# A two-part transformer in one launch: all steps placed anew, with one reader per PSUM bank and powers in gaps of VectorE; 14 identity transposes in place of 32

## The chip, the core and the metric

The kernel runs on one core of one Trainium2 chip. The metric is the device time of one launch in microseconds (us). The kernel before takes 2158.5 us in the median of three runs (2158.13 to 2163.83).

## What is computed

Two blocks follow each other on the same 512 tokens of width 1024, all in float32. Cut to what matters:

```python
# first block, layer 0: differential attention beside a memory attention
h = rms_norm(x, a_norm); q, k, v, qm, gate = split(h @ a_w_in)
q, k = rope(rms_norm(q)), rope(rms_norm(k))            # per head of 64
o = (softmax(q0 k0') - lam * softmax(q1 k1')) @ v      # causal, 6 heads of 128
x = x + (concat(rms_norm(o), mem_attention(qm, mem)) * silu(gate)) @ a_w_out
# first block, layer 1: stick-breaking attention, 12 heads of 64
k, v = split(rms_norm(x, kv_norm) @ w_kv_shared); q, qm, gate = split(rms_norm(x, b_norm) @ b_w_in)
x = x + (concat(stick_breaking(q, k, v), mem_attention(qm, mem)) * silu(gate)) @ b_w_out
# second block, two layers of the same form
proj = rmsnorm(x) @ w_in                               # 1024 to 12 parts
y_a = gmlp_spatial(u, v) * silu(z_a)
y_b = mla_attention(c_q, c_kv, k_rope) * silu(z_b)     # 8 heads, latent queries and keys
y_c = rg_lru(x_c) * silu(z_c)                          # convolution, two gates, a scan over time
m = sigmoid(g_a)*(y_a @ w_proj_a) + sigmoid(g_b)*(y_b @ w_proj_b) + sigmoid(g_c)*(y_c @ w_proj_c)
x = x + rmsnorm(m @ w_out)
```

## The kernel before

**Products.** Every float32 matrix is split into a rounded part and the rest (`split`: `hi` is a copy that rounds, `lo` is the source less `hi`), and each product is three matmuls, hi by hi, hi by lo and lo by hi (`mm3`). Weights come by DMA in chunks of 512 KB or less into the arena `fa` (float32), are split there into the arena `ra` (the rounded type), and are then used; the split is a copy on ScalarE or VectorE and a subtraction on VectorE (`wchunk`, `dense_fm`, `dense_tm`, `dense_tk`). The arena `sm` holds small columns. The eight PSUM banks are `ps0` to `ps7`.

**Steps.** A block is a set of named steps, run in the order of a list: in the first layer `q0` to `q2` are the three groups of queries and keys, `v0` and `v1` the values (with the memory's queries in `v1`), `h0` to `h5` the heads, `k0` and `k1` the memory's keys and values of both layers, `a0` the memory attention, `n0` the norm over the heads, `g0` to `g7` the gates, `f0` to `f7` the gated products. In the second layer `p0` to `p5` are pairs of heads. In the second block `Q0` makes the rotated parts of all eight heads' queries, `T0` to `T7` are the heads, `Z`, `G`, `z` gates, `R` the recurrence, and `A`, `B`, `D` the three projections.

**Order.** Nothing is issued while the steps run: `Sched.record` only notes each operation, with what it reads and writes. `Sched.place` then goes through a model of five engines with costs written out by hand (`cost`) and gives each engine, whenever it is free in the model, the first operation that is ready, so that the order on all engines, the tiles' places in memory, and for operations marked with `any` also the engine (a copy on ScalarE or VectorE, a product of two tiles on VectorE or GpSimd) come out of it. Tables steer it: the step lists `plan_a`, `plan_b`, `plan_l`, `plan_l1`; how far ahead of the oldest unfinished operation a step may begin (`reach_*`, `window*`); how much earlier its weights may be asked for (`lead_*`); and `spare` (PSUM banks kept free), `hold`, `early`, `depth`, `patience`. `Sched.issue` emits the result, so nearly every instruction of a profile bears the one line 571 (line 600 in the changed kernel), and rows are told apart by tiles and shapes. What waits on what is set by the real dependencies: two engines that read one PSUM bank read it one after the other.

**Details that the change touches.** Where heads are normalised (`head_norm_T`), the reciprocal root is a power on GpSimd (`rpow`), and the result goes through TensorE transposes against the identity (`identr`, `ident`, tiles `rc` and `ident`). `pairs_T` stores transposed pairs of heads, the even head of each pair in one half of the partitions. At the very start 32 transposes of the identity onto itself keep TensorE busy while the first loads are under way.

Of the kernel before, what the change touches and what calls it, by code (L numbers as in the profile page):

```python
# [19 lines left out]
P = 128  # L20
# [9 lines left out]
class VTile:  # L30

    __slots__ = ("kind", "units", "cols", "at", "uses", "first", "last", "busy")

    def __init__(self, kind, units, cols):
        self.kind, self.units, self.cols = kind, units, cols
        self.at, self.uses, self.first, self.last, self.busy = None, 0, None, None, 0.0


class VAP:
# [119 lines left out]
class Sched:  # L161

    plan_l = "q0 k0 Q0 V0 N0 N1 T0 T1 Z1 T2 Z0 T3 N3 V1 N2 T4 T5 Z5 Z2 C0 Z4 Z3 T6 Z6 T7 Z7 B1 W0 X0 R1 R0 " \
        "B7 G1 G4 X1 B0 G2 G3 B2 W1 R2 G0 R3 B6 B4 B3 M0 S0 G5 G9 G6 B5 G7 M1 G8 P1 P6 D0 D7 P5 P2 P0 " \
        "z2 z0 D3 D4 P7 D5 P4 P3 z1 z3 z7 u1 u2 z4 z5 D6 z6 u0 u3 D2 u5 u6 u7 u4 A3 A6 A4 A2 A0 D1 A7 " \
        "A5 A1"
    reach_l = {'A': 1200, 'B': 300, 'D': 300, 'M': 350, 'P': 150, 'Q': 600, 'R': 1200, 'T': 200, 'V': 600, 'Z':
        800, 'u': 400, 'z': 500}  # L170
    plan_l1 = "k0 q0 V0 Q0 N1 N0 N2 T0 T2 T1 Z1 V1 Z0 N3 T6 Z2 T4 T5 Z5 T3 Z3 T7 C0 Z7 Z4 X0 Z6 W0 R1 B1 R0 " \
        "G2 M0 W1 B0 G3 B2 G1 X1 R2 B3 G4 G0 S0 B6 R3 B4 B7 G5 B5 M1 G6 P4 G7 G9 G8 D6 P3 P0 P2 D5 P7 " \
        "z2 D4 P6 z6 P1 P5 u6 z3 z4 D0 z0 u2 z5 u0 u3 u5 z7 D7 z1 u1 D1 u7 D2 u4 A5 A1 A2 D3 A6 A3 A0 " \
        "A7 A4"
    reach_l1 = {'A': 500, 'D': 150, 'M': 600, 'N': 250, 'P': 300, 'Q': 350, 'R': 150, 'S': 100, 'T': 50, 'X': 400,
        'q': 250, 'z': 1200}
    patience = 2500
    window_a = 169
    window = 169
    window_b = 200  # L180
    window_l = 298
    pool_n = 256
    reach_n = 94
    reach_x = 49
    spare = 1
    hold = 24
    early = 100
    late_x = (0, 40, 520)
    last = 1
    plan_a = "c0 q0 q2 v0 h0 h1 k0 q1 v1 g2 h2 h3 g1 h5 g6 h4 g7 n0 a0 g4 f6 f1 g0 f0 f2 f7 f4 g5 f5 g3 k1 " \  # L190
        "f3"
    plan_b = "v0 q0 p0 q1 p1 q2 m0 q3 a0 q4 q5 p2 g7 p4 g2 g1 g4 p5 g0 g6 p3 g3 g5"
    reach_a = {'a': 100, 'c': 50, 'f': 2000, 'g': 250, 'h': 50, 'm': 2250, 'n': 400, 'q': 600, 'v': 400}
    reach_b = {'a': 100, 'g': 400, 'm': 250, 'p': 400, 'q': 300}
    depth = 64
    lead_a = {'a': 20, 'f': 120, 'h': 800, 'k': 20, 'q': 120, 'v': 200}
    lead_b = {'a': 200, 'g': 120, 'm': 200, 'p': 300, 'q': 40, 'v': 500}
    lead_l = {'A': 80, 'C': 800, 'G': 200, 'P': 120, 'S': 500, 'T': 80, 'W': 200, 'X': 200, 'Z': 120, 'u': 40, 'z': 800}
    lead_l1 = {'A': 200, 'B': 80, 'D': 800, 'G': 800, 'R': 80, 'T': 80, 'X': 200, 'Z': 300, 'k': 20, 'u': 80, 'z': 80}

    def __init__(self, nc, mems):
        self.nc, self.mems = nc, mems
# [181 lines left out]
    def place(self):  # L384
# [55 lines left out]
        def pick(e, t):  # L440
            h, held, late, found = ready[e], [], None, None
            while h and len(held) < self.depth:
                x = heapq.heappop(h)
                op = ops[x[1]]
                if op.start is not None:
                    continue
                if op.idx > front + op.reach:
                    held.append(x)
                    if op.idx > front + 1500:
                        break  # L450
                    continue
# [12 lines left out]
                found = op  # L464
                break
# [25 lines left out]
        while done < len(ops):  # L491
# [11 lines left out]
            if what == "ready":  # L503
                enlist(x)
            elif what == "done":
                fin[x] = 1
                if x == front:
                    while front < len(ops) and fin[front]:
                        front += 1
                    moved = True  # L510
            elif what == "give":
                mems[x.kind].give(x)
                freed.add(x.kind)
            if events and events[0][0] <= t:
                continue
            for kd in (parked if moved else freed):
# [8 lines left out]
            for e in engs:  # L525
# [14 lines left out]
                op.start, op.eng = t, e  # L540
# [6 lines left out]
                ends[op.idx] = end  # L547
                push(end, "done", op.idx)
                done += 1
                for s in op.succ:  # L550
                    so = ops[s]
                    so.left -= 1
                    if so.left == 0:
                        so.ready = max(ends[d] + self.lat(ops[d].eng, so.alts[0][0]) for d in so.deps)
                        push(so.ready, "ready", so)
                for v in op.vts:
                    v.uses -= 1
                    v.busy = max(v.busy, end)
                    if v.uses == 0:
                        push(v.busy + 150, "give", v)  # L560
        self.span = t
        return order

# [55 lines left out]
class Kern:  # L619
# [80 lines left out]
    def consts(self):  # L700
# [178 lines left out]
    def pairs_T(self, dst, src):  # L879
# [54 lines left out]
    def mem_attention(self, qT, kT, vm):  # L934
# [4 lines left out]
        for p in range(2):  # L939
            o = self.p()  # L940
            for hh in range(2):
                lo = 64 * hh
                pT = self.r(2, 512)
                for u in range(2):
                    sc = self.p(2, 256)
                    for i in range(2):
                        for x in range(2):
                            self.mm(sc[:, i, :], qT[:, 2 * p + hh, tok(2 * u + i)], kT[x][:, 2 * p + hh, :], x == 0, x == 1)
                    m, sm = self.s(2), self.s(2)
                    nc.vector.tensor_reduce(m, sc, axis=AX.X, op=ALU.max)  # L950
                    nc.vector.tensor_scalar(m, m, -0.125, None, op0=ALU.mult)
# [444 lines left out]
    def latent(self, l, A, w, hT, lhs):  # L1396
# [427 lines left out]
```

## Time and profile before

| | value |
|---|---|
| median of three runs | 2158.5 us |
| profiled execution, its own time | 2162.5 us |
| profiled execution, its span | 2160.7 us |
| TensorE (PE) busy | 2121.9 us of the span |
| VectorE (DVE) busy | 1427.7 us |
| ScalarE (ACT) busy | 939.1 us |
| GpSimd (POOL) busy | 87.8 us |
| TensorE's granted clock, mean | 0.996 of full |

A page of the profile describes one profiled execution. A row of a group gives the line, the engine, the operation, the tiles written and read, how often, the busy time and the mean length of one, and then the idle time ahead of these instructions with what ended it. "PE ps <- DVE ra" among the waits means that TensorE stood until VectorE had written a tile of `ra`. In a table by stretch the clock column is the share of TensorE's full clock that was granted.

### The profile page before, as it was taken

Reading aid. Unit: us, or ns where it says so; the run is one execution under the profiler, and the core shown is the slowest. Engines: PE = TensorE matmul, PEld = TensorE weight load, DVE = VectorE, ACT = ScalarE, POOL = GpSimd, SP = SyncE. Lnnn points to the kernel's source line nnn. Section 1 sums busy time; section 2 is a strip of 40 time slices with the busy share of each in tenths; the row PEclk is TensorE's granted clock in tenths of the full one; section 3 lists DMA queues with packets and bytes.
Section 4 is the critical chain, followed back from the end, with each engine's and each line's share of the span. In section 5 each row is a group of like instructions: output and inputs, shape, how many; then the busy total and the mean of one; then the engine's idle time right before and its main releaser. Section 6 shows DMA issues by size and latency. Waiting matters only on the chain.

```text
span 2160.7 us, 27498 instructions
## 1 busy us (share of the span) xinstructions
PE 2121.9 (98%) x10191; PEld 1764.0 (82%) x10191; DVE 1427.7 (66%) x2761; ACT 939.1 (43%) x1706; POOL 87.8 (4%) x94
## 2 busy tenths in 40 slices
PE   9999999999999999999999999999999999999998
PEld 7877788788898888888888888888878888888887
DVE  7678966778777777874635434687886676553343
ACT  5546633555445546563412122445655454122321
POOL 1220000000010000000100000100000000000000
PEclk9999999999999999999999999999999999999999
DMA  5431353552553033633424542521435254244442
GB/s 165 117 95 52 123 182 85 129 133 73 168 146 83 12 100 104 169 93 103 124 70 126 153 138 92 173 75 38 128 87 143 76 143 124 73 141 122 134 137 78
DMA packets 325245, 243.51 MB, mean 113 GB/s; under 512 B 22565, under 2 KB 278389, under 8 KB 324726
## 3 DMA queue, kind: packets, MB, share of 16 engines
q1 hardware_dynamic: 325110, 241.75, 39.1%
q8 instruction: 80, 1.31, 0.2%
q14 instruction: 55, 0.45, 0.1%
HBM read 205.26 MB, written 16.78 MB: 103 GB/s over the span
## 4 chain that ended last, share of the span: by engine, by line
PE 63%; DVE 3%; ACT 1%; DMA 1%; issue 0%; POOL 0%; SPq 0%; DVEq 0%; POOLq 0%; ACTq 0%
PE ps L571 63%; DVE fa L571 2%; DVE ra L571 1%; ACT ra L571 0%; ACT fa L571 0%; DMA fa<-in_w_in 0%; DMA ra<-ra 0%; POOL sm L571 0%; DMA fa<-in_gate_x 0%; SPq L571 0%; DVE sm L571 0%; DVEq L1820 0%; POOLq L1820 0%; ACTq L571 0%; DVEq L571 0%
## 5 line engine op out<-in xcount | busy, mean ns | idle before, releaser
L571 PE MATMUL ps<-ra 128*128 128x512 f32 (+3 forms) x9308 | 2061.5, 379 | 14.3 <-DVE ra L571 8.8
L571 PEld LDWEIGHTS ps<-ra 128*128 128x128 f32 x9308 | 1667.1, 189 | 331.6 <-DVE ra L571 18.5
L571 DVE TENSOR_TENSOR ra<-fa,ra 128x1024 fp32r<-128x1024 f32 (+5 forms) x479 | 488.4, 1036 | 194.4 <-ACT ra L571 104.3
L571 ACT CAST ra<-fa 128x1024 fp32r<-128x1024 f32 (+4 forms) x401 | 358.6, 912 | 358.3 <-DVE fa L571 152.5
L571 ACT ACTIVATE fa<-ps 128x512 f32<-128x512 f32 (+2 forms) x244 | 133.1, 573 | 354.7 <-PE ps L571 337.1
L571 ACT CAST ra<-ps 128x384 fp32r<-128x384 f32 (+5 forms) x266 | 119.9, 469 | 193.5 <-PE ps L571 183.1
L571 DVE TENSOR_TENSOR ra<-ps,ra 128x512 fp32r<-128x512 f32 (+5 forms) x330 | 160.5, 507 | 46.5 <-ACT ra L571 40.2
L571 DVE SCALAR_TENSOR_TENSOR fa<-fa,ps 128x512 f32<-128x512 f32 x116 | 79.2, 685 | 152.2 <-PE ps L571 103.5
L571 POOL TENSOR_TENSOR sm<-sm,mhalf 128x1 f32<-128x1 f32 (+2 forms) x76 | 75.8, 1001 | 1249.2 <-DVE sm L571 1145.0
L571 PE MATMUL ps<-ident,fa 128*128 128x128 f32 x679 | 113.6, 279 | 11.1 <-DVE fa L571 10.1
L571 PEld LDWEIGHTS ps<-ident,fa 128*128 128x128 f32 x679 | 83.0, 142 | 42.5 <-DVE fa L571 19.4
L571 DVE TENSOR_TENSOR fa<-fa 128x512 f32<-128x512 f32 (+5 forms) x169 | 102.1, 615 | 13.1 <-ACT fa L571 11.1
L571 ACT ACTIVATE fa<-fa,sm 128x256 f32<-128x256 f32 (+3 forms) x151 | 82.7, 555 | 35.3 <-DVE sm L571 30.1
L571 DVE SCALAR_TENSOR_TENSOR fa<-ps,cols,fa 128x256 f32<-128x256 f32 (+4 forms) x140 | 75.8, 578 | 31.5 <-PE ps L571 18.4
L571 DVE TENSOR_TENSOR fa<-fa,ps 128x512 f32<-128x512 f32 (+1 forms) x44 | 30.2, 686 | 67.2 <-PE ps L571 66.3
L571 ACT ACTIVATE fa<-fa 128x512 f32<-128x512 f32 (+3 forms) x93 | 55.5, 605 | 39.1 <-DVE fa L571 25.6
L567 ACT ACT_TABLE_LOAD x47 | 60.3, 1283 | 1.5 <-PEq L1812 0.7
L571 ACT ACTIVATE fa<-ps,cols 128x512 f32<-128x512 f32 x60 | 41.6, 718 | 43.9 <-PE ps L571 34.0
L571 DVE SCALAR_TENSOR_TENSOR fa<-fa 128x512 f32<-128x512 f32 x76 | 51.2, 689 | 12.4 <-ACT fa L571 11.4
L571 DVE SCALAR_TENSOR_TENSOR fa<-fa,sm 128x512 f32<-128x512 f32 (+3 forms) x80 | 50.6, 649 | 12.3 <-POOL sm L571 11.7
L571 DVE CAST ra<-fa 128x1024 fp32r<-128x1024 f32 (+4 forms) x83 | 45.0, 545 | 19.1 <-PE ps L571 10.2
L571 DVE TENSOR_TENSOR fa<-ps,fa 128x512 f32<-128x512 f32 (+3 forms) x64 | 25.6, 436 | 46.2 <-ACT fa L571 46.0
(80 smaller groups left out, 658.6 us busy)
## 6 DMA issues: line engine op xcount, KB each, us to landing
fa<-in_w_in SPq DMA_DIRECT2D x152, 512.0 KB, 4.6
ra<-ra SPq DMA_DIRECT2D x72, 128.0 KB, 2.3
fa<-in_a_w_in SPq DMA_DIRECT2D x16, 512.0 KB, 5.7
fa<-in_b_w_in SPq DMA_DIRECT2D x16, 512.0 KB, 6.2
fa<-in_w_proj_b SPq DMA_DIRECT2D x16, 512.0 KB, 3.7
dr_mg<-fa SPq DMA_DIRECT2D x32, 256.0 KB, 2.3
fa<-in_w_proj_c SPq DMA_DIRECT2D x16, 512.0 KB, 4.0
fa<-dr_mg SPq DMA_DIRECT2D x32, 256.0 KB, 3.8
```

Source lines behind the costliest of these rows:

```text
L567: self.nc.scalar.preload_act_table_set(op)
L571: f(*[self.bound(y) for y in a], **{n: self.bound(y) for n, y in k.items()})
```

## The change

1. **The model of the order.** `VTile` gets a field `seen`, the end of the last read by VectorE and by ScalarE. When ScalarE or VectorE looks for work, an operation on a PSUM tile that the other one is still reading is put off until that read has ended. A power on GpSimd begins in the model only when VectorE's port is free (`begin`, `end`), not when GpSimd is.
2. **The tables** are all new: step lists, reaches, leads, `spare` 1 to 3, `patience` 2500 to 1500, `depth` 64 to 100, and others. So the order on every engine, the choice of engine for `any` operations, and the places in memory change.
3. **Pairs of heads**: in `pairs_T` the even heads of all pairs are stored first, then the odd ones; the two readers (`mem_attention`, `attend`) index accordingly.
4. **Start**: 14 transposes of the identity in place of 32.

The number of other matmuls does not change.

```diff
-    reach_a = {'a': 100, 'c': 50, 'f': 2000, 'g': 250, 'h': 50, 'm': 2250, 'n': 400, 'q': 600, 'v': 400}
+    reach_a = {'a': 100, 'c': 50, 'g': 250, 'h': 50, 'k': 150, 'm': 2250, 'n': 300, 'q': 500, 'v': 400}
...
-    spare = 1
+    spare = 3
...
@@ Sched.place, pick
+                if e in ("ACT", "DVE"):
+                    w = max((v.seen[e == "ACT"] for v in op.vts if v.kind == "p"), default=0.0) + 135
+                    if w > max(t, 135):
+                        push(w, "tick", None)
+                        held.append(x)
+                        continue
...
+            elif what in ("begin", "end"):
+                if port > t:
+                    push(port + 15, what, x)
+                elif what == "begin":
+                    push(t + next(y for y in x.alts if y[0] == "POOL")[5], "end", x)
...
-        for _ in range(32):
+        for _ in range(14):
             nc.tensor.transpose(busy, self.ident, self.ident)
...
-            d = dst[:, o // 64::2, :]
+            d = dst[:, n * (o // 64):n * (o // 64 + 1), :]
...
-                            self.mm(sc[:, i, :], qT[:, 2 * p + hh, tok(2 * u + i)], kT[x][:, 2 * p + hh, :], x == 0, x == 1)
+                            self.mm(sc[:, i, :], qT[:, p + 2 * hh, tok(2 * u + i)], kT[x][:, p + 2 * hh, :], x == 0, x == 1)
```

How the order moves, at three places.

**TensorE, third group of queries and keys (`q1`), beside the second half of the values (`v1`).** The rows with `rc` are the transposes of the normalised heads, four to a bank; the 128x512 rows are products. Before:

```order
L571 MATMUL ps_68<-rc,ra 128x128 x2
L571 MATMUL ps_67<-ident,fa 128x128 x2
L571 MATMUL ps_68<-rc,ra 128x128 x2
L571 MATMUL ps_72<-ra 128x512 x7
L571 MATMUL ps_66<-rc,ra 128x128 x4
L571 MATMUL ps_72<-ra 128x512
L571 MATMUL ps_73<-ident,fa 128x128 x2
L571 MATMUL ps_72<-ra 128x512 x3
L571 MATMUL ps_69<-ra 128x512 x12
L571 MATMUL ps_68<-ra 128x512 x6
L571 MATMUL ps_67<-ra 128x512
L571 MATMUL ps_71<-rc,ra 128x128 x4
```

Now:

```order
L600 MATMUL ps_68<-ra 128x512 x5
L600 MATMUL ps_71<-ident,fa 128x128 x2
L600 MATMUL ps_67<-ra 128x512 x6
L600 MATMUL ps_68<-ra 128x512
L600 MATMUL ps_73<-ra 128x512
L600 MATMUL ps_69<-ra 128x512 x6
L600 MATMUL ps_73<-ra 128x512 x5
L600 MATMUL ps_67<-ra 128x512 x6
L600 MATMUL ps_69<-ra 128x512
L600 MATMUL ps_66<-rc,ra 128x128 x4
L600 MATMUL ps_69<-ra 128x512 x3
L600 MATMUL ps_70<-rc,ra 128x128 x4
```

The transposes stood among the products from early on; now more products stand ahead of the first, and the groups follow each other closely.

**VectorE, end of `v1` and the weights of gate `g2`.** `COPY fa<-ps 128x256` is the copy of one tile's memory queries, `TENSOR_TENSOR ra<-fa,ra 128x1024` the `lo` part of the gate's weights. Before:

```order
L571 TENSOR_TENSOR ra<-ps_72,ra 128x256
L571 TENSOR_REDUCE sm<-fa 128x4
L571 TENSOR_SCALAR sm<-sm 128x4
L571 COPY fa<-ps_69 128x256
L571 TENSOR_TENSOR ra<-ps_69,ra 128x256
L571 TENSOR_REDUCE sm<-fa 128x4
L571 TENSOR_TENSOR fa<-fa,sm 128x256
L571 TENSOR_SCALAR sm<-sm 128x4
L571 COPY fa<-ps_68 128x256
L571 TENSOR_TENSOR ra<-ps_68,ra 128x256
L571 TENSOR_REDUCE sm<-fa 128x4
L571 TENSOR_TENSOR ra<-fa,ra 128x1024
```

Now:

```order
L600 TENSOR_TENSOR ra<-ps_68,ra 128x256
L600 TENSOR_REDUCE sm<-fa 128x4
L600 TENSOR_SCALAR sm<-sm 128x4
L600 TENSOR_TENSOR ra<-ps_73,ra 128x256
L600 TENSOR_REDUCE sm<-fa 128x4
L600 TENSOR_TENSOR fa<-fa,sm 128x256
L600 TENSOR_SCALAR sm<-sm 128x4
L600 TENSOR_TENSOR ra<-ps_67,ra 128x256
L600 TENSOR_REDUCE sm<-fa 128x4
L600 TENSOR_SCALAR sm<-sm 128x4
L600 TENSOR_TENSOR fa<-fa,sm 128x256
L600 TENSOR_TENSOR ra<-fa,ra 128x1024
```

The copies out of PSUM are gone from VectorE; ScalarE has them.

**VectorE, end of the first layer: memory keys `k1` behind gate `g3`.** `TENSOR_TENSOR ra<-ps 128x4x128` is the `lo` part of the transposed memory, for which TensorE waits. Before:

```order
L571 TENSOR_SCALAR sm<-sm 128x1 x2
L571 CAST ra<-zcol 128x4x64 x2
L571 CAST ra<-fa 128x1024
L571 TENSOR_TENSOR ra<-fa,ra 128x512
L571 SCALAR_TENSOR_TENSOR fa<-fa,sm 128x512
L571 TENSOR_TENSOR ra<-fa,ra 128x1024 x2
L571 SCALAR_TENSOR_TENSOR fa<-fa,ps_67 128x512
L571 TENSOR_TENSOR ra<-ps_68,ra 128x4x128
```

Now:

```order
L600 CAST ra<-fa 128x512
L600 TENSOR_TENSOR ra<-fa,ra 128x512
L600 SCALAR_TENSOR_TENSOR fa<-fa,sm 128x512
L600 TENSOR_TENSOR sm<-sm 128x1
L600 TENSOR_SCALAR sm<-sm 128x1
L600 TENSOR_TENSOR ra<-fa,ra 128x1024
L600 SCALAR_TENSOR_TENSOR fa<-fa,ps_66 128x512
L600 TENSOR_TENSOR ra<-ps_69,ra 128x4x128
```

Ahead of that `lo` part one subtraction of 1024 columns stands where two stood, and the copy of 1024 columns has left VectorE.

## Rows read from the trace of the kernel before

**Rows 1.** The page: busy time, share and instructions of each engine.
```profile
PE 2121.9 (98%) x10191; PEld 1764.0 (82%) x10191; DVE 1427.7 (66%) x2761; ACT 939.1 (43%) x1706; POOL 87.8 (4%) x94
```

**Rows 2.** By stretch: us, busy time (instructions) by engine, clock, DMA share, GB/s.
```profile
0.00:285.00 285.00, 270.52 (x1333) 215.17 (x1334) 228.59 (x613) 162.80 (x359) 40.26 (x33) 0.98 0.41 120
285.00:570.00 285.00, 273.86 (x1458) 230.30 (x1457) 215.98 (x402) 141.57 (x293) 8.57 (x10) 0.99 0.42 114
```

**Rows 3.** Waits of TensorE, whole span: us in total, times, longest.
```profile
PE ps L571 <- DVE ra L571: 12.9, 17, 1.8
PE ps L571 <- DVE fa L571: 11.1, 18, 2.8
```

**Rows 4.** Instructions in order of time, start: start, length, count, [idle before, releaser].
```profile
1.36 6.09 PE L571 MATMUL ps<-ident 128*128 128x128 f32 x32 [1.36 <-POOL ident masks.py:199]
...
9.43 1.05 ACT L571 CAST ra<-fa 128x1024 fp32r<-128x1024 f32 x1 [1.62 <-DMA fa<-in_a_w_in]
...
11.63 2.55 PE L571 MATMUL ps<-ra 128*128 128x512 f32 x7 [0.45 <-ACT ra L571]
```

**Rows 5.** TensorE in the first 13 us: busy (matmuls), granted clock, DMA share, GB/s.
```profile
1.30:6.30 5.00, 4.94 (x23) 1.00 0.83 237
6.40:7.40 1.00, 1.00 (x11) 1.00 0.88 241
9.70:13.10 3.40, 2.96 (x12) 0.50 1.17 320
```

**Rows 6.** In order of time, 68 to 84 us: powers, and transposes behind one.
```profile
68.66 1.73 POOL L571 TENSOR_TENSOR sm<-sm,mhalf 128x8 f32<-128x8 f32 x1 [1.16 <-DVE sm L571]
...
73.59 5.69 POOL L571 TENSOR_TENSOR sm<-sm,mhalf 128x8 f32<-128x8 f32 x1 [3.20 <-DVE sm L571]
...
83.43 0.80 PE L571 MATMUL ps<-rc,ra 128*128 128x128 f32 x7 [1.33 <-DVE ra L571]
```

**Rows 7.** Waits of TensorE in 40 to 155 us.
```profile
PE ps L571 <- DVE ra L571: 4.1, 5, 1.6
PE ps L571 <- DVE fa L571: 1.0, 1, 1.0
```

**Rows 8.** TensorE in 166 to 174 and 269 to 273 us: busy, granted clock, DMA.
```profile
166.50:170.10 3.60, 1.77 (x8) 1.00 0.30 86
170.10:173.50 3.40, 3.40 (x10) 0.50 0.00 0
...
269.00:272.50 3.50, 3.50 (x13) 0.51 0.68 219
```

**Rows 9.** In order of time, 162 to 170 us: a copy, gate weights, TensorE.
```profile
162.63 0.42 DVE L571 COPY fa<-ps 128x256 f32<-128x256 f32 x1 [4.88 <-ACT ra L571]
...
167.84 1.22 DVE L571 TENSOR_TENSOR ra<-fa,ra 128x1024 fp32r<-128x1024 f32 x1
...
169.11 1.25 PE L571 MATMUL ps<-ra 128*128 128x512 f32 x4 [1.83 <-DVE ra L571]
```

**Rows 10.** In order of time, 265 to 269 us: VectorE's splits and TensorE.
```profile
265.29 2.35 DVE L571 TENSOR_TENSOR ra<-fa,ra 128x1024 fp32r<-128x1024 f32 x2
...
268.90 0.64 PE L571 MATMUL ps<-ra 128*128 128x512 f32 x1 [1.40 <-DVE ra L571]
```

**Rows 11.** A group by form, and TensorE's waits in 640:670 and 1430:1447 us.
```profile
L571 DVE CAST ra<-ps 64x512 fp32r<-64x512 f32 x8 | 5.5, 692 | 1.0 <-ACT ra L571 0.9
...
PE ps L571 <- DVE fa L571: 1.0, 3, 0.4
...
PE ps L571 <- DVE fa L571: 1.3, 3, 0.6
```

**Rows 12.** In order of time, 490 to 497 us: ScalarE behind a load, TensorE.
```profile
490.99 1.05 ACT L571 CAST ra<-fa 128x1024 fp32r<-128x1024 f32 x1 [2.05 <-DMA fa<-in_b_w_in]
...
496.44 0.63 PE L571 MATMUL ps<-ident,fa 128*128 128x128 f32 x4 [2.77 <-DVE fa L571]
```

**Rows 13.** A DMA issue row: count, KB each, median us to landing.
```profile
fa<-in_w_in SPq DMA_DIRECT2D x152, 512.0 KB, 4.6
```

More of the change, by code (lines that the diff above doesn't have):

```diff
@@ L30 @@
 class VTile:
-    __slots__ = ("kind", "units", "cols", "at", "uses", "first", "last", "busy")
+    __slots__ = ("kind", "units", "cols", "at", "uses", "first", "last", "busy", "seen")
     def __init__(self, kind, units, cols):
@@ L161 @@
 class Sched:
[L165 to L177, printed above, removed]
@@ L178 @@
-    window_a = 169
-    window = 169
-    window_b = 200
+    plan_l = "k0 q0 Q0 V0 N0 N1 T1 T0 Z1 T2 Z0 N2 T3 V1 T4 T5 Z5 Z2 N3 Z4 Z3 T6 Z6 T7 C0 Z7 B1 W0 X0 R1 R0 " \
+        "B7 G4 G3 X1 B6 G1 G2 B2 B0 W1 R2 B3 G0 B4 M0 R3 B5 G9 S0 G5 G6 G7 M1 G8 D7 P1 P2 P6 P5 D0 P7 " \
+        "P0 P3 z2 D3 z0 z1 D4 P4 z7 z3 z4 u2 u1 z5 z6 u0 D6 u3 D2 u6 u5 u4 u7 A6 A4 A0 A3 D5 D1 A7 A2 " \
+        "A1 A5"
+    reach_l = {'A': 300, 'B': 300, 'M': 350, 'P': 2000, 'Q': 500, 'R': 250, 'T': 200, 'V': 600, 'Z': 800, 'u':
+        400, 'z': 400}
@@ new lines @@
+    plan_l1 = "k0 q0 V0 Q0 N1 N0 T1 T0 T2 Z1 Z0 N2 N3 V1 T6 C0 Z2 T4 T5 Z5 T3 Z3 T7 X0 Z7 Z6 W0 R0 R1 Z4 B1 " \
+        "B0 G2 W1 M0 B2 G3 G1 X1 R2 B3 G0 B6 R3 S0 G4 B5 B7 G5 G8 B4 M1 G6 P2 G7 P6 P4 G9 D6 P3 P0 D5 " \
+        "P7 z2 z6 z0 z4 P1 D4 u0 P5 D1 u6 z3 D0 z5 D7 u3 u5 z7 z1 u4 u2 u7 D2 u1 A5 A2 D3 A3 A7 A0 A4 " \
+        "A6 A1"
+    reach_l1 = {'A': 400, 'B': 300, 'D': 100, 'M': 600, 'N': 350, 'P': 500, 'Q': 350, 'R': 150, 'S': 100, 'T': 50,
+        'X': 400, 'q': 250, 'z': 100}
+    patience = 1500
@@ L181 @@
+    window_a = 143
+    window = 143
+    window_b = 246
     window_l = 298
     pool_n = 256
-    reach_n = 94
-    reach_x = 49
-    spare = 1
+    reach_n = 162
+    reach_x = 43
+    spare = 3
     hold = 24
-    early = 100
-    late_x = (0, 40, 520)
+    early = 200
+    late_x = (0, 70, 650)
     last = 1
-    plan_a = "c0 q0 q2 v0 h0 h1 k0 q1 v1 g2 h2 h3 g1 h5 g6 h4 g7 n0 a0 g4 f6 f1 g0 f0 f2 f7 f4 g5 f5 g3 k1 " \
+    plan_a = "c0 q0 q2 v0 h0 h1 k0 q1 v1 g2 h3 h2 g1 g6 h4 h5 g7 n0 a0 f1 g4 g0 f7 f6 f2 f4 f0 g5 f5 g3 k1 " \
@@ L199 @@
-    lead_l1 = {'A': 200, 'B': 80, 'D': 800, 'G': 800, 'R': 80, 'T': 80, 'X': 200, 'Z': 300, 'k': 20, 'u': 80, 'z': 80}
+    plan_b = "v0 q0 p0 q1 p1 q2 m0 q3 a0 q5 q4 p2 g7 g1 p4 g2 g0 p5 g4 g6 p3 g5 g3"
+    reach_a = {'a': 100, 'c': 50, 'g': 250, 'h': 50, 'k': 150, 'm': 2250, 'n': 300, 'q': 500, 'v': 400}
+    reach_b = {'a': 100, 'g': 400, 'p': 600, 'q': 300, 'v': 200}
+    depth = 100
+    lead_a = {'c': 200, 'f': 500, 'g': 40, 'h': 80, 'k': 20, 'n': 500, 'q': 120, 'v': 200}
+    lead_b = {'a': 120, 'm': 40, 'p': 20, 'q': 20, 'v': 800}
@@ L201, in __init__ @@
+    lead_l = {'A': 40, 'C': 800, 'G': 20, 'P': 120, 'S': 500, 'T': 80, 'W': 200, 'X': 200, 'Z': 20, 'u': 40, 'z': 80}
+    lead_l1 = {'A': 120, 'B': 80, 'G': 120, 'N': 20, 'P': 40, 'R': 500, 'T': 500, 'X': 200, 'Z': 200, 'k': 80, 'u': 80, 'z': 80}
     def __init__(self, nc, mems):
@@ L475, in pick, with finish @@
             return found
+        def finish(op, end):
+            nonlocal done
+            ends[op.idx] = end
+            push(end, "done", op.idx)
+            done += 1
+            for j in op.succ:
+                so = ops[j]
+                so.left -= 1
+                if so.left == 0:
+                    so.ready = max(ends[d] + self.lat(ops[d].eng, so.alts[0][0]) for d in so.deps)
+                    push(so.ready, "ready", so)
+            for v in op.vts:
+                v.uses -= 1
+                v.busy = max(v.busy, end)
+                if v.kind == "p" and op.eng in ("ACT", "DVE"):
+                    v.seen[op.eng == "DVE"] = max(v.seen[op.eng == "DVE"], end)
+                if v.uses == 0:
+                    push(v.busy + 150, "give", v)
         def elsewhere(op, e, t):
@@ L513, in place @@
                 freed.add(x.kind)
+            elif what in ("begin", "end"):
[3 more added lines that the diff above has]
+                    push(t + next(y for y in x.alts if y[0] == "POOL")[5], "end", x)
+                else:
+                    free["POOL"] = t
+                    push(t, "tick", None)
+                    finish(x, t)
             if events and events[0][0] <= t:
@@ L532, in place @@
                 end = t + alt[5]
+                op.start, op.eng = t, e
+                if e == "POOL" and 0 < alt[6] < alt[5]:
+                    order.append((t, op, alt))
+                    free[e] = np.inf
+                    push(max(t, port), "begin", op)
+                    continue
                 if alt[6]:
@@ L539, in place @@
                     end += 1283
-                op.start, op.eng = t, e
                 order.append((t, op, alt))
@@ L546, in place @@
                     end = dma = max(dma, hwdge + 650) + max(op.bytes / 290.0, 100)
[L547 to L560, printed above, removed]
+                finish(op, end)
         self.span = t
```

11 lines of the change are left out of this document (3 added, 8 removed).

## The prediction

> **What bounds the kernel now.** I read the engines' totals first. TensorE is busy for 2121.9 us [rows 1] of a span of 2160.7, VectorE for two thirds of it, so only 38.8 us of idle TensorE and its slow stretches can be won. By stretch, 14.5 us of the idle time (285.00 less 270.52) lie in the first layer and 11.1 in the second [rows 2]; the remaining 1590 us hold 13.2. TensorE's waits then give the cause: 12.9 us for tiles that VectorE writes into `ra`, 11.1 for tiles in `fa` [rows 3]. They are 35 waits, none over 2.8 us, so no single one decides. Besides, the granted clock falls to 0.5 for stretches of 3.4 us (1.2 in place of 2.4 GHz). Two of these, at 170.1 and 269.0, begin just behind such a wait [rows 8]; each takes half of 3.4, some 1.7 us.
>
> The number of products stays. The change can move time in three ways: shorter waits, fewer clock falls, fewer transposes at the start.
>
> **Start.** Of 32 transposes, which last 6.09 us from 1.36 on [rows 4], 18 go. In the first 5 us 23 of them take 0.217 each [rows 5], so 18 free 3.9 us of TensorE. But the first product, at 11.63, waits for something else: ScalarE's copy of the first weights begins when their DMA lands, at 9.43, and lasts 1.05 [rows 4]. The load does not come earlier by this change, so the product cannot start before 10.48, and the gain is 1.15 at most; I take 1.0. Against it stands the clock: the first products already run at 0.5 until 13.1 [rows 5]. With fewer transposes ahead of them the slow stretch may end later. Its price lies between 0 and a whole stretch, 1.7; I take 0.5, since only the 1.0 us of products that move ahead are surely slow. The start brings 0.5, from -1.7 to 1.15.
>
> On this the Trainium skill speaks ("TensorE: Matmul & The Clock Gate", "Part 4: PE-mode transpose"): transposes do not count as busy time and do not bring the full clock. In the trace 23 identity transposes take 5.0 us and the next 11 take 1.0, with nothing else ahead of them [rows 5], so here they did bring the faster rate. By the page the 0.5 for the clock would vanish and the sum be 0.5 us higher.
>
> **First layer, queries and keys.** A power of 128x8 on GpSimd takes 1.73 us in a calm place and 5.69 beside VectorE's uninterrupted splits; behind the latter the transposes wait 1.33 [rows 6]. In 40 to 155 us, where these heads are normalised, TensorE loses 4.1 and 1.0 us, 5.1 in all [rows 7]. The new order does two things there. The powers are placed where VectorE is free, and in TensorE's order the `q1` transposes stand behind about 95 products after their last own product, where 65 stood. A matmul takes 0.21 us on the mean (2121.9 / 10191, [rows 1]), so thirty more are some 6 us, longer than the difference of 4.0 between the two powers. That would cover all of it, but the transposes of one group now also stand closer together, each waiting for VectorE's split of its own tile. I take it that two of the six waits stay: 5.1 x 4 / 6 = 3.4; bounds 0 and 5.1.
>
> **Gate `g2`.** TensorE waits 1.83 us at 169.11 for the `lo` part of the gate's weights, which VectorE ends at 169.06 [rows 9]. Of the copies out of PSUM ahead of it, 0.42 each, three are gone from VectorE's order: 3 x 0.42 = 1.3, bounds 0 and 1.8. The clock falls right behind this wait [rows 8]. Whether a wait of 0.5 still lets it fall no row tells; I take half of 1.7, 0.85 (0 to 1.7).
>
> **Memory keys `k1`.** TensorE waits 1.40 at 268.90 behind two subtractions of together 2.35 [rows 10]. One stands there now: 1.2 (0 to 1.4), and half of the fall at 269.0, 0.85 (0 to 1.7).
>
> **Rotated queries `Q0`.** Eight casts of 64x512 on VectorE, 0.69 each, go to ScalarE, four in each layer of the second block; TensorE's waits for the tiles there are 1.0 and 1.3 us [rows 11]. ScalarE's copy must still come ahead of VectorE's subtraction, so I take two thirds, 1.5 of 2.3. The even-first storage costs nothing by itself: as many elements are written and the same matmuls read them.
>
> **Pair `p2`.** TensorE waits 2.77 at 496.44 for a scan on VectorE whose input came late: ScalarE had stood 2.05 for a weights' DMA [rows 12] before it turned to the exponentials. SP's order asks for that load some five products earlier, 5 x 0.21 = 1.1 us; I take that, bounds 0 and 2.8.
>
> **What it adds.** The copies that leave VectorE load ScalarE by as much (39 of them); it is busy 939.1 us [rows 1], so on the whole they hide in its idle time. A copy that comes behind a weights' copy waits 1.05 [rows 4]. Where a bank's second reader is put off, nothing new is waited for on the chip: two engines read a bank one after the other already. GpSimd's powers stand in the same queue as before; one begun later delays its own head's transposes alone. The real risk is the loads. Many leads are smaller, and in the second layer of the second block one load of `G` is asked for only some eleven products, 2.3 us, ahead of its first use, while such a load lands 4.6 us behind its issue [rows 13] and is copied in 1.05. Such a place costs 4.6 + 1.05 - 2.3 = 3.4, with a clock fall 5.1. But by the semaphores this load needs only an earlier DMA, so it may be issued as soon as SP comes to it, well ahead. New waits of all kinds: I take 1.0; bounds 0 and 5.1 for one place.
>
> **Sum.** 0.5 + 3.4 + 1.3 + 0.85 + 1.2 + 0.85 + 1.5 + 1.1 - 1.0 = 9.7 us. The profiled execution took 2162.5 us, 4.0 over the median; 2162.5 - 9.7 = 2152.8 on its scale, and on the median's 2158.5 - 9.7 = 2148.8. That is 0.45%. What is late next: the waits at the memory attention and the other pairs of heads stay nearly as they are, as their surroundings in the order do. All gains at their upper bounds, without new waits: 1.15 + 5.1 + 1.8 + 1.7 + 1.4 + 1.7 + 2.3 + 2.8 = 18, or 2140.5. All at their lower: +1.7 + 5.1 = 6.8 more, 2165.3.
>
> **Rivals.** *The waits only move.* VectorE still does all subtractions, and a tile that leaves its place in the queue sooner lets TensorE reach the next dependency sooner. For it: 35 small waits at many places, all behind the same engine. Then the start and a quarter of the other gains (10.2) remain, 0.5 + 2.55 - 1.0 = 2.05: 2156.4. Chance 0.27.
>
> *Slower: weights land late.* The mechanism is that of the load of `G` above, at other places too: with shorter leads a load lands after TensorE has reached its first product. Each place costs 5.1 with its clock fall. It decides from the third place on (15.3 - 10.7 of gains = 4.6 lost) and passes the bound of 0.3% from the fourth: 20.4 - 10.7 = 9.7, 2168.2. Against it: among TensorE's waits VectorE's two rows hold 24.0 of 38.8 us [rows 3], so loads come in time now nearly everywhere. Chance 0.10.
>
> *More than the forecast.* If the clock falls and most waits in the first two layers go (25.6 us idle, two thirds of it 17, and two more falls 3.4), the gain is some 20: 2138. For it: powers and readers are placed by what the chip shows. Against it: two thirds of the waits in 285 to 570 have nearly the same order around them. Chance 0.11.
>
> **Numbers.** The forecast, 2148.8, has 0.52. A measurement of this kernel tells about 0.3% from no change, 6.5 us: faster is below 2152.0, slower above 2165.0. The forecast case lies below 2152 in four fifths, the large gain wholly, the moved waits in a fifth: 0.42 + 0.11 + 0.06 = 0.59. Slower holds most of its rival and little else, 0.09; the rest, 0.32, is the same. The range leaves out half of the large gain and most of the slower case: 2138 to 2161.
>
> **What would show it.** Right: in the trace of the changed kernel, TensorE's wait for `ra` in 40 to 155 us is under 2.5 us; no power there lasts near 5; the first product stands at about 10.6; the wait ahead of `g2` is about 0.5 and the clock column stays at 1.00 behind it and behind `k1`; no cast of 64x512 stands on VectorE; idle TensorE is about 29 us. Wrong: the same totals of waits at other tiles (waits that moved); waits for DMAs of `in_w_in` in the second block (late weights); a first stretch of low clock that reaches beyond 14 us.

## The result

The changed kernel takes 2136.7 us in the median (2135.83 to 2137.49), beside 2160.3 for the kernel before on the same chip: a ratio of 0.9889, 95% interval 0.9872 to 0.9906. It is 23.6 us (1.1%) faster. The forecast was 9.7 us faster, with a range that ended at 2138; the time lies 1.3 us below it. The direction was right, the size was not: two and a half times the forecast. The time is that of the rival "more than the forecast" (2138), to which the prediction gave 0.11, but not by its account: it took two thirds of the 25.6 us of idle time out of the first two layers, some 17, where 10.6 went. That the two numbers agree is in part luck.

### The profile after

The profiled execution has a span of 2135.3 us, 25.4 less than before. The page's first line, to be read beside [rows 1]:

```profile
PE 2111.3 (99%) x10173; PEld 1762.2 (83%) x10173; DVE 1410.7 (66%) x2730; ACT 952.7 (45%) x1740; POOL 82.7 (4%) x91
```

The stretches with the same work as those of [rows 2] end at 274.9 and 553.2 us now (us; then busy time and instructions of PE, PEld, DVE, ACT, POOL; clock; DMA share; GB/s):

```profile
0.00:274.90 274.90, 266.44 (x1314) 211.69 (x1315) 225.76 (x598) 164.14 (x370) 38.26 (x32) 1.00 0.40 121
274.90:553.20 278.30, 271.85 (x1458) 230.56 (x1457) 212.08 (x393) 148.03 (x308) 9.64 (x10) 0.99 0.44 120
553.20:2135.30 1582.10, 1572.98 (x7404) 1319.94 (x7402) 972.91 (x1741) 640.51 (x1063) 34.82 (x49) 1.00 0.39 112
```

TensorE's idle time fell from 14.5 to 8.5, from 11.1 to 6.5 and from 13.2 to 9.1 us: in all three, from 38.8 to 24.0 together. The stretches themselves became 10.1, 6.7 and 8.6 us shorter. Its waits, to be read beside [rows 3]:

```profile
PE ps L600 <- DVE ra L600: 6.4, 10, 1.4
PE ps L600 <- DVE fa L600: 3.0, 6, 1.3
```

Thirty-five waits for VectorE with 24.0 us have become sixteen with 9.4. But 14.8 us less idle time is not 25.4 us. The rest shows only in the start times of the matmuls. Two products at the end of the first layer, and a dense row of fifteen for comparison (start, length, count, idle time before and what ended it):

```profile
258.39 0.48 PE L600 MATMUL ps<-ra 128*128 128x512 f32 x1
259.42 1.92 PE L600 MATMUL ps<-ra 128*128 128x512 f32 x6 [0.55 <-ACT ra L600]
...
476.83 3.64 PE L600 MATMUL ps<-ra 128*128 128x512 f32 x15
```

A product alone has a record of 0.48 us, but in a dense row the starts lie (3.64 - 0.48) / 14 = 0.23 apart. At 258.39 it takes 1.03 us to the next start, so 0.80 are lost, where the view says 0.55. Summed over the whole trace behind the start, the kernel before loses 40.1 us in 61 waits whose recorded idle time is 29.6; the changed one 19.4 us in 31 waits with 14.0. So the waits bring 20.7 us. Three stretches behind the start at half clock (1.2 GHz) became one, at 388.1 us, behind three short waits of 0.40, 0.57 and 0.73: 3.1. Matmuls elsewhere bring another 3.9, and the start loses some 2.2.

### The profile page after: what moved, and what is told of

The parts are those of the page before. It is cut to its first block, busy times and chain, and to the rows that moved or that the text cites. A ratio compares the mean times of both kernels' runs of the same rounds, so it can differ in the third digit from the quotient of the medians.

```text
span 2135.3 us, 27479 instructions
## 1 busy us (share of the span) xinstructions
PE 2111.3 (99%) x10173; PEld 1762.2 (83%) x10173; DVE 1410.7 (66%) x2730; ACT 952.7 (45%) x1740; POOL 82.7 (4%) x91
## 4 chain that ended last, share of the span: by engine, by line
PE 77%; DVE 3%; DMA 1%; issue 0%; ACT 0%; SPq 0%; DVEq 0%; POOLq 0%; POOL 0%; ACTq 0%
PE ps L600 77%; DVE fa L600 2%; DVE ra L600 1%; DMA fa<-in_b_w_in 0%; DMA fa<-in_w_in 0%; DMA ra<-ra 0%; ACT fa L600 0%; ACT ra L600 0%; SPq L600 0%; DVEq L1849 0%; POOLq L1849 0%; POOL sm L600 0%; DVE sm L600 0%; DVEq L600 0%; ACTq L1849 0%
## 5 line engine op out<-in xcount | busy, mean ns | idle before, releaser
L600 PE MATMUL ps<-ra 128*128 128x512 f32 (+4 forms) x9308 | 2054.6, 379 | 10.3 <-DVE ra L600 5.8
L600 ACT CAST ra<-fa 128x1024 fp32r<-128x1024 f32 (+6 forms) x408 | 363.0, 909 | 339.4 <-DVE fa L600 154.5
L600 ACT CAST ra<-ps 128x512 fp32r<-128x512 f32 (+5 forms) x296 | 132.2, 466 | 171.0 <-PE ps L600 166.0
L600 DVE TENSOR_TENSOR ra<-ps,ra 128x384 fp32r<-128x384 f32 (+5 forms) x330 | 161.0, 505 | 59.1 <-ACT ra L600 52.4
L600 DVE TENSOR_TENSOR fa<-fa 128x512 f32<-128x512 f32 (+6 forms) x169 | 102.2, 613 | 24.0 <-ACT fa L600 22.1
L600 PEld LDWEIGHTS ps<-ident,fa 128*128 128x128 f32 x679 | 83.7, 142 | 33.3 <-DVE fa L600 8.3
L600 ACT ACTIVATE fa<-fa 128x512 f32<-128x512 f32 (+2 forms) x90 | 53.6, 606 | 45.2 <-DVE fa L600 27.3
L600 DVE CUSTOM_DVE_ANT_0 fa<-ps,fa 128x128 f32<-128x128 f32 (+3 forms) x112 | 52.4, 483 | 6.8 <-PE ps L600 6.6
```

Of the source, the lines that this page charges most:

```text
L600: f(*[self.bound(y) for y in a], **{n: self.bound(y) for n, y in k.items()})
```

## The experiments

Some keep an order row by row and change one thing in it; in the others the model places a new one.

### The transposes at the start

```diff
  # order of the changed kernel, each of the 14 transposes issued 2 or 3 times
...
+                if seen <= 14:
+                    for _ in range(32 // 14 + (seen <= 32 % 14)):
...
  # order of the kernel before, 18 of the 32 left out
...
+                if seen <= 32:
+                    for _ in range(14 // 32 + (seen <= 14 % 32)):
...
```

> The changed kernel, its order kept instruction by instruction, but 32 identity transposes issued at the start in place of 14. Clock theory: after 14 transposes TensorE's matmuls still run at half rate (0.427 us for 512 columns) until 15.3 us, and the stage that begins at 29.2 us in the kernel before begins at 31.4; with 32 the transposes turn to 0.109 us each near 6.2 us as before, half rate lasts to about 13, and about 2.2 us come back: 2136.7 - 2.2 = 2134.5. Rival, that the first weights and their split set the start whatever the clock: the transposes only stand in the way, 2136.7 to 2138.5.

> The kernel before with its order kept, but 14 identity transposes in place of 32. Clock theory: slower by about 2.2 us at the start, 2162.5 where the kernel before takes 2160.3, half rate until about 15. The step of the prediction (gain 1.0, less 0.5 for the clock): 2159.8. Rival of the weights: no change.

With 32 the changed kernel takes 2137.0 (0.9897, 0.988 to 0.9913), with 14 the kernel before takes 2159.0 (0.9999, 0.999 to 1.0009). Neither moved by anything that these times can tell. The clock theory's 2.2 us do not come; the 0.5 of the prediction is too small to be seen in a time. The traces see it: behind the start the same four transposes begin at 25.21 with 14 and at 25.53 with 32 in the order before, at 26.37 and 26.85 in the changed order, so the 18 bring 0.3 and 0.5 us. TensorE's first instructions in the changed kernel, with two of VectorE's, then with 32 transposes in its order, then the kernel before with 14:

```profile
1.36 3.25 PE L600 MATMUL ps<-ident 128*128 128x128 f32 x14 [1.36 <-POOL ident masks.py:199]
4.54 3.77 PE L600 MATMUL ps<-fa 1*128 1x512 f32 x4
...
9.30 0.69 DVE L600 CAST ra<-fa 128x1024 fp32r<-128x1024 f32 x1
...
10.14 0.76 PE L600 MATMUL ps<-ra 128*128 128x512 f32 x1
...
10.62 1.22 DVE L600 TENSOR_TENSOR ra<-fa,ra 128x1024 fp32r<-128x1024 f32 x1
...
11.89 2.93 PE L600 MATMUL ps<-ra 128*128 128x512 f32 x6 [0.98 <-DVE ra L600]
```

```profile
1.36 5.76 PE L605 MATMUL ps<-ident 128*128 128x128 f32 x32 [1.36 <-POOL ident masks.py:199]
7.04 1.98 PE L607 MATMUL ps<-fa 1*128 1x512 f32 x4
...
12.48 2.93 PE L607 MATMUL ps<-ra 128*128 128x512 f32 x6 [1.17 <-DVE ra L607]
```

```profile
4.54 3.77 PE L578 MATMUL ps<-fa 1*128 1x512 f32 x4
9.12 1.97 PE L578 MATMUL ps<-ident,fa 128*128 128x128 f32 x8 [0.81 <-DVE fa L578]
11.03 6.69 PE L578 MATMUL ps<-ra 128*128 128x512 f32 x24
```

The four products of one row take 1.98 us behind 32 transposes and 3.77 behind 14: most of what the missing transposes free, the half rate of the next matmuls takes back. The start is set elsewhere. In the changed kernel VectorE copies the first weights (9.30), one product runs at 10.14, and all others wait until 11.89 for the second half of the split (10.62, 1.22 us long), where the kernel before has seven products from 11.63 on without a gap [rows 4]. That is the order's doing, and its loss of about 2 us remains whatever the transposes. Half rate has a part in it: it lasts to 16.0 and 15.8 us in the two traces of the changed order and to 13.1 in the two of the order before. Its end differs between executions of one order, though; the run with the old pairs below has it at 18.5.

The prediction cites the Trainium skill ("TensorE: Matmul & The Clock Gate", "Part 4: PE-mode transpose") for transposes that do not bring the full clock. The traces here disagree again: 14 take 3.25 us, 32 take 5.76, so the later 18 take 0.14 each where the first take 0.23.

### Copies of g2 and Q0 alone

```diff
  # move: the numbers of three copies ahead of g2 and of eight of Q0
...
+            if op.idx in move:
+                alt = next(y for y in op.alts if y[0] == "ACT")
...
```

> The kernel before with its order kept, but eleven copies out of PSUM given from VectorE to ScalarE at their places: three of the memory queries ahead of the weights of g2, eight of the rotated queries Q0. The terms of the prediction: at 169 us the wait of 1.83 falls to about 0.5 and the low clock behind it may go (1.3 and 0 to 1.7), the waits of Q0 (1.0 and 1.3) fall to a third (1.5): 2160.3 - 2.8 to - 4.5 = 2155.8 to 2157.5. Rival, that who copies doesn't matter since the subtraction of the same bank must follow the copy anyway: the waits stay, within 1 us of the kernel before.

Measured: 2157.5 (0.999, 0.998 to 1.0001), 1.8 us down by the medians and at the edge of what can be told. The places can be read, though. VectorE and TensorE at `g2` with the copies moved, and its waits at `Q0`, in 636:668 us and again, with the same row, in 1424:1444:

```profile
164.50 0.42 DVE L574 TENSOR_TENSOR ra<-ps,ra 128x256 fp32r<-128x256 f32 x1 [0.58 <-ACT fa L574]
...
167.96 1.42 PE L574 MATMUL ps<-ra 128*128 128x512 f32 x5 [1.23 <-DVE ra L574]
```

```profile
PE ps L574 <- DVE fa L574: 0.4, 2, 0.2
```

The waits of `Q0` fall from 2.3 [rows 11] to 0.8 us, the 1.5 of the prediction. That of `g2` falls from 1.83 [rows 9] to 1.23 only: half of the copies' 1.3, since VectorE now stands idle (0.58 in the row, 0.36 ahead of the next such split) until ScalarE has read the bank.

### With and without the two rules of the model

```diff
  # without the reader rule
-                if e in ("ACT", "DVE"):
+                if False:
...
  # without the rule of the powers
-                if e == "POOL" and 0 < alt[6] < alt[5]:
+                if False:
```

> The changed kernel with its new tables, 14 transposes and new pairs, but the order placed by the old model: without the rule of one reader per bank and without that of the powers. Theory of readers: second readers stand in their engine's queue behind the first again (39 us of such idle time on ScalarE and VectorE before, 17 after, by bank and engine in the traces), TensorE's idle time returns to 35 us or more: 2152 to 2165. Theory of the tables (the search over tables found the gain, the rules are bystanders): 2140 or less. Theory of a lucky order: any fresh order loses alike, told apart by the next runs.

> The changed kernel with its new tables and the rule of one reader per bank, but without the rule of the powers. About 5100 of some 5840 rows of the order differ from the changed kernel's, as many as without both rules. Theory that the reader rule carries the gain: near the changed kernel's 2136.7, up to 2145. Theory that the powers carry it: near 2171, as without both rules. Theory of a lucky order (any other order under these tables loses alike): also near 2171.

> Control: the changed kernel with both rules and all tables, but the model's 450 ns between two DMA issues set to 440, which moves about 4450 rows of the order and says nothing of readers or powers. Theory of the rules: 2137 to 2147. Theory of a lucky order: 2155 or more.

> Second control: as the changed kernel, but a power that finds VectorE's port taken looks again after 40 ns of the model in place of 15; about 5000 rows of the order move. Theory of the rules: 2137 to 2147. Theory of a lucky order: 2155 or more.

> Second order without both rules under the new tables: as the earlier kernel without them (2171.4), with 640 in place of 650 ns in the model's DMA; about 3400 rows differ from it. Theory of readers: again 2160 to 2176, reader idle near 39 us, TensorE's waits for fa near 17. If 2171 was one unlucky order: 2145 to 2152, as the orders with the rule.

> The new tables with the rule of the powers and without the rule of one reader per bank (and 440 in place of 450 ns between two DMA issues in the model, with which the order can be placed). Theory of readers: as without both rules, 2164 to 2176, idle time of ScalarE and VectorE behind the other reader near 39 us. Theory that either rule does it, as they move the same copies: 2145 to 2155.

> The changed kernel with the reader rule kept for the first block alone and put off for the second. Theory of readers: the first block (to about 556 us) within 3 us of the changed kernel, unless the long wait of p2 comes back (1.3 us in the changed kernel, 6.0 in both controls); the second block loses what the rule gives there, by stage in the traces some 7 to 9 us: 2143 to 2147, or 2150 to 2155 with p2.

The kernel before and its relatives:

> Control on the kernel before: its own tables and model, 32 transposes, old pairs, but 440 in place of 450 ns between two DMA issues in the model; about 5400 of some 5900 rows of the order move. If the order that a search has picked under a model is worth some 10 us against another order of the same model (2136.7 against 2147 to 2151 under the new one), this takes 2168 to 2180, idle time behind a bank's other reader stays near 39 us. If the tables alone set the time, 2158 to 2164.

> Second such control on the kernel before: 640 in place of 650 ns from a DMA's issue to its start in the model, about 2100 rows move. Picked order: 2165 to 2180. Tables alone: 2158 to 2164.

> The tables of the kernel before, with the reader rule in the model, 14 transposes and the new pairs, without the rule of the powers. Theory of readers: faster than the kernel before, 2140 to 2152, though the tables were not made for the rule. Theory of the tables: they were made for the old model, so any new order loses: 2160 to 2175.

The table puts them together. "Reader idle" is worked out from traces and order: for each PSUM bank that ScalarE and VectorE read one behind the other, neither needing the other's result, the idle time that ends with the other's read. Waits, idle time and loss are TensorE's behind the start, as above; a half-clock stretch is 3.4 or 6.8 us long. "`p2`" is TensorE's wait at that pair, and "second block" the time from TensorE's 7402nd matmul before the end to the end, in the traces. The kernel before took 2159.3 to 2161.3 in the median beside these runs.

| tables, rules | reader idle | waits | their idle time | lost in them | half-clock stretches | `p2` | second block | time |
|---|---|---|---|---|---|---|---|---|
| new, both rules (the changed kernel) | 17.3 | 31 | 14.0 | 19.4 | 1 | 1.3 | 1581.9 | 2136.7 |
| new, both, 440 ns between DMAs | 19.4 | 35 | 21.1 | 27.4 | 1 | 6.0 | 1583.5 | 2146.9 |
| new, both, powers look after 40 ns | 19.2 | 36 | 23.0 | 29.4 | 4 | 5.4 | 1583.9 | 2150.9 |
| new, readers alone | 18.2 | 38 | 21.9 | 28.8 | 1 | 4.1 | 1582.4 | 2149.2 |
| new, both, readers in the first block alone | 25.0 | 43 | 19.2 | 26.6 | 1 | 1.4 | 1590.0 | 2145.6 |
| new, powers alone (440 ns) | 39.8 | 61 | 32.4 | 42.9 | 3 | 4.9 | 1589.6 | 2169.8 |
| new, neither | 38.7 | 68 | 36.3 | 48.0 | 2 | 6.4 | 1592.0 | 2171.4 |
| new, neither (640 ns to a DMA's start) | 38.8 | 65 | 34.3 | 45.4 | 3 | 6.1 | 1590.6 | 2172.1 |
| old, neither (the kernel before) | 39.0 | 61 | 29.6 | 40.1 | 3 | 2.8 | 1590.8 | 2160.3 |
| old, neither, 440 ns | 39.1 | 61 | 33.3 | 43.8 | 3 | 6.0 | 1589.6 | 2167.0 |
| old, neither, 640 ns | 38.6 | 60 | 29.0 | 39.2 | 2 | 2.8 | 1589.6 | 2162.4 |
| old, readers alone | 18.0 | 39 | 31.7 | 38.7 | 6 | 6.0 | 1590.7 | 2166.3 |

Intervals of the ratio are about 0.0015 to either side. TensorE's waits for VectorE without both rules, and then with the reader rule alone:

```profile
PE ps L600 <- DVE fa L600: 17.5, 19, 6.4
PE ps L600 <- DVE ra L600: 12.9, 20, 1.4
```

```profile
PE ps L600 <- DVE fa L600: 10.1, 9, 4.1
PE ps L600 <- DVE ra L600: 7.2, 12, 1.4
```

Three things follow. First, under the new tables the reader rule is worth about 20 us: without it three orders take 2170 to 2172, with it three orders other than the changed kernel's take 2147 to 2151, two of them 4 us above what was expected; the first order without both rules came out 6 above its range as well. In the second block it is worth 8.9 of that (2145.6 against 2136.7), as expected, and there it hangs on no single order: all four new orders with the rule take 1581.9 to 1583.9 for that block, all four without it there 1589.6 to 1592.0.

Second, the rule of the powers does not carry it: with powers alone the time is that of neither rule, and without it that of the controls. Nor did it make the powers short; in the changed kernel a 128x8 power lasts 2098 ns in the mean, before 2247, and 1688 with the new tables and neither rule:

```profile
L600 POOL TENSOR_TENSOR sm<-sm,mhalf 128x8 f32<-128x8 f32 x12 | 25.1, 2098 | 54.9 <-DVE sm L600 42.3 <-issue 12.3 <-DVE fa L600 0.3
```

Third, the rule alone is not the gain. Under the old tables it halves the reader idle as well and takes 22 waits away, but the remaining ones are long, with six half-clock stretches, and the time of 2166.3 is that of the fresh order without the rule (2167.0); its second block, 1590.7, gains nothing. The theory of readers expected 2140 to 2152 there and was wrong. Rule and tables bring the gain together; which entries of the tables the rule needs stays open, as do runs of each with tables made anew for it.

The control of 640 ns on the old tables missed the range for a picked order and lies in that for tables that set the time alone: it moved 2100 rows and hardly anything in the waits. That of 440 ns came out 1 us below the range for a picked order. So how much an order picked by search is worth differs from one control to the other; the next section shows at what place.

### Why the changed kernel is 10 us better than its neighbours

Between the changed kernel and the first control most lies in one place: the same work takes 52.8 us (465.8 to 518.6) in one and 59.4 (467.0 to 526.4) in the other, 6.6 of the 9.4 us between the two traces. ScalarE and TensorE at pair `p2` in the changed kernel, then in the control, there with DMAs that SP issues:

```profile
476.31 1.05 ACT L600 CAST ra<-fa 128x1024 fp32r<-128x1024 f32 x1 [0.55 <-DMA fa<-in_b_w_in]
...
481.76 0.63 PE L600 MATMUL ps<-ident,fa 128*128 128x128 f32 x4 [1.29 <-DVE fa L600]
```

```profile
472.76 6.69 SPq L600 DMA_DIRECT2D ra<-ra  x10
...
482.17 1.04 ACT L600 CAST ra<-fa 128x1024 fp32r<-128x1024 f32 x1 [5.26 <-DMA ra<-ra]
...
483.86 2.08 ACT L600 ACTIVATE fa<-ps 128x512 f32<-128x512 f32 x4
...
487.62 1.09 PE L600 MATMUL ps<-ident,fa 128*128 128x128 f32 x4 [6.00 <-DVE fa L600]
```

The copy is that of gate weights `g0`. In the control it waits 5.26 us at the head of ScalarE's queue for DMAs from `ra` to `ra`, and the two copies and four exponentials of `p2` stand behind it. In the changed kernel it waits 0.55, for its own weights. The likely reason is another place in `ra`; the rows do not name places, so that is not shown. To show that the copy holds up `p2`, it was issued behind those six operations, all else kept:

```diff
  # the copy is set aside here and issued after six more of ScalarE's
...
+            if op.idx == 4132:
+                wait, left = (f, a, k), 6
+                continue
...
```

> The first control (440 ns between DMA issues, 2146.9), order and places kept, but one copy on ScalarE, of gate weights g0, issued behind the six operations of pair p2 that stood behind it. Theory that the copy blocks them: TensorE's wait of 6.0 us at 487 us falls to 1 or less and the kernel takes 2140 to 2142. Rival, that the exponentials wait for something else or the wait only moves on to the gate: 2146 to 2147.

> The changed kernel with the same copy issued behind the same six operations. Its wait at p2 is 1.3 us, of which the copy takes 1.05 on ScalarE: 2135.4 to 2136 if the gate's products don't wait for the copy instead, 2136.7 to 2138 if they do.

The control falls from 2146.9 to 2139.1 (0.9898, 0.9882 to 0.9915). Its rows there:

```profile
481.57 0.63 PE L610 MATMUL ps<-ident,fa 128*128 128x128 f32 x4 [0.32 <-DVE fa L610]
481.62 1.05 ACT L606 CAST ra<-fa 128x1024 fp32r<-128x1024 f32 x1 [2.31 <-DMA ra<-ra]
```

The copy still waits, but TensorE no longer does for long. So the changed kernel's order is some 2 us better than this neighbour; the rest of its lead was this one copy. In the two other neighbours the wait of `p2` is 5.4 and 4.1 us; there the edit was not tried. In the first of them, the one with 40 ns, the copy of `g0` is not held up, but a split on VectorE is:

```profile
487.86 1.35 DVE L600 TENSOR_TENSOR ra<-ps,ra 128x256 fp32r<-128x256 f32 x3 [5.00 <-DMA ra<-ra]
...
492.19 1.09 PE L600 MATMUL ps<-ident,fa 128*128 128x128 f32 x4 [5.38 <-DVE fa L600]
```

The same kind of wait stands in all eight orders of the table whose `p2` is above 4 us, with the reader rule and without it: ScalarE or VectorE stands 3.6 to 6.0 us there for a DMA from `ra` to `ra`. The orders of the two kernels, and the two that stay close to them, have 1.3 to 2.8 us. So every fresh order here loses at `p2` whatever the rule, and the rule's 20 us come on top.

In the changed kernel the same edit takes the wait from 1.29 to 0.3 us, and the kernel 2136.9 (0.9892, 0.9877 to 0.9907): no difference that can be told. No version here is clearly faster than the changed kernel.

### The pairs of heads

```diff
-            d = dst[:, n * (o // 64):n * (o // 64 + 1), :]
+            d = dst[:, o // 64::2, :]
...
```

> The changed kernel with the pairs of heads stored in turn as before; every engine's order stays the same row by row. The prediction's step (storage costs nothing and brings nothing by itself): 2136.7 within 2 us. Rival, that contiguous halves are written faster: each of 64 stores of 64x512 some 0.05 us longer and a part of it on the path, 2138.5 to 2141.

Measured: 2137.6 (0.9893, 0.9876 to 0.9909). The stores of 64x512 on VectorE with the pairs in turn (the changed kernel's row is the same):

```profile
L600 DVE TENSOR_TENSOR ra<-ps,ra 64x512 fp32r<-64x512 f32 x16 | 11.0, 689 | 0.3
```

The storage costs and brings nothing by itself that can be told, as the prediction had it.

## The prediction, point by point

**What bounds the kernel** was right in kind: small waits for VectorE at many places. The price was wrong. The prediction took the recorded idle time for what a wait costs; 61 waits with 29.6 us of it cost 40.1. On the mean a wait term of the sum was a quarter too small for this alone.

**Start**, 0.5 us gained. Wrong: about 2.2 lost. The step that failed is what the first products wait for. The prediction took ScalarE's copy of the first weights, with a bound of 10.48. In the kernel before, the wait ended with a later operation of ScalarE, its copy of the transposed input out of PSUM (the first of these two operations):

```profile
11.01 1.05 ACT L571 CAST ra<-ps 128x512 fp32r<-128x512 f32 x2
```

In the changed kernel the weights' copy is on VectorE, one product starts at 10.14, below the bound, and the next six wait until 11.89, for a split that the new order puts later. The transposes by themselves bring 0.3 and 0.5 us in the traces, about the net 0.5 of the prediction; but it kept the order of the first products as it was. (The 18 transposes free 6.09 - 3.25 = 2.8 us, not 3.9, since the last ones run at the faster rate; the sum did not use this.)

**Queries and keys**, 3.4 of 5.1. The waits of [rows 7] became this one row in 40 to 153 us:

```profile
PE ps L600 <- DVE ra L600: 0.8, 2, 0.5
```

So 4.3 recorded: two waits stay, as the prediction took it, but short ones. Shorter powers are not the reason. The longest in that stretch, 5.69 before, is still 4.36:

```profile
46.48 4.36 POOL L600 TENSOR_TENSOR sm<-sm,mhalf 128x8 f32<-128x8 f32 x1 [0.28 <-DVE fa L600]
```

The greater distance of the `q1` transposes and fewer reader stalls remain. In the three orders with the new tables and without the reader rule, waits of 1.3 to 2.2 us are left in 40 to 155 us; in the five with it, 0.7 to 2.6. So some 3 of the 4.3 came with the tables, and what the rule adds here can't be told.

**g2**, 1.3 and half a clock fall. The wait is 0.66 us now, with a new one of 0.52 ahead of it, for ScalarE, which has the copies now:

```profile
164.09 0.43 PE L600 MATMUL ps<-ident,fa 128*128 128x128 f32 x2 [0.52 <-ACT fa L600]
165.18 2.11 PE L600 MATMUL ps<-ra 128*128 128x512 f32 x8 [0.66 <-DVE ra L600]
```

The net is 0.65, or 0.45 with a wait of 0.20 at 167.48; that the moved copies would put VectorE behind ScalarE was missing from the step. The clock did not fall here, but this is no gift of the shorter wait: in the kernel before with 14 transposes the wait is unchanged and the clock stays up behind it.

```profile
167.92 1.41 PE L578 MATMUL ps<-ra 128*128 128x512 f32 x5 [1.83 <-DVE ra L578]
```

```profile
167.90:171.30 3.40, 3.36 (x15) 1.00 0.00 0
```

**k1**, 1.2. Of the wait of 1.40 [rows 10] nothing over 0.14 us is left: right. The wait for ScalarE's copy of the same tile ahead of it stays (0.44 before, 0.55 at 259.42 now). Its clock fall is gone too, with the same reservation.

**Q0**, 1.5. The 2.3 us of [rows 11] are 0.4 in the changed kernel: 1.9, and the experiment on the copies gave 1.5. **p2**, 1.1: 2.77 became 1.29, so 1.5; ScalarE's wait for the load there fell from 2.05 to 0.55, as the step had it. But that nothing else held up `p2` is luck of this order: its neighbours wait 4.1 to 6.0 us there.

**New waits**, 1.0 lost. Behind the start nearly none: 1.0 for ScalarE at 230 us stands in place of 1.5 for VectorE there, and 1.0 for a DMA at 821 in place of 1.4 at 1596. No load came late: the place of the load of `G` shows nothing, and the slower rival had nothing to stand on.

**What is late next.** This is the step that failed and cost most. The prediction priced the longest waits and left the others as they are, because the order around them looked alike. The named places give 4.3 + 0.65 + 1.3 + 1.9 + 1.5 = 9.7 us of recorded idle time, against 8.5 forecast; but 15.6 went behind the start (29.6 to 14.0). Some 5.9 us came from waits that the sum did not hold, in the second layer, the recurrence and the other pairs. The second block shows it most plainly: the sum held 1.5 us for it, and it became 8.6 shorter. The reader rule acts on the whole kernel: 39.0 us in which ScalarE or VectorE stood for a bank's other reader became 17.3. The prediction saw two engines read "one after the other already" and concluded that putting a reader off costs nothing; it did not ask what the engine does in the time that it no longer stands.

In short: recorded idle at the named places 9.7, at others 5.9, what the records hide 5.1 (20.7 less 15.6), clock falls 3.1, other matmuls 3.9, start -2.2: 25.5 for a span that is 25.4 shorter. The cause of the 3.9 was not looked into, and which clock falls an execution has was not settled: the same order shows them at other places, or not. Of the signs that the prediction named, the wait for `ra`, the 64x512 casts (none is left on VectorE), `g2` and the clock came; idle TensorE is 24.0 us and not 29, and a power of 4.36 us remains.

## What to carry to other kernels

Price a wait of TensorE from the start of the matmul ahead of it to the start of the next, less the dense distance, not by the idle time of the record. When a planner learns a rule of the chip, count the whole class of stalls that the rule is about, not the longest few; and run neighbours of the order (one constant of the model moved by a few per cent) before the gain is put down to the rule, since one blocked copy at the head of a queue was worth 8 us here. Copies that wait for a DMA belong behind the work that doesn't.

## What was not expected of the hardware

At the start of the changed kernel the granted clock stands at 1.00 in the view while six products take 2.93 us: (2.93 - 0.76) / 5 = 0.43 from start to start, where a dense row has 0.23. The first record of the clock in this trace lies at 16.0 us; ahead of it the starts of the matmuls are what tells:

```profile
9.70:13.10 3.40, 2.42 (x7) 1.00 0.96 315
```

DMAs from `ra` to `ra`, of 128 KB each, hold up what waits for them for long. In the control SP takes 6.69 us to issue ten of them from 472.76 on, 0.67 each; between 460 and 490 us such a DMA lands 2.2 to 5.0 us behind its issue, and the copy of `g0` stands until 482.
